# A hybrid encoder block on one core: the last product of the SwiGLU in parts of 3, 4, 4 pairs, x joined by accumulating DMA, and the final norm's two factors applied in one operation

## The chip, the cores and the metric

The kernel runs on one core of one Trainium2 chip. The metric is the device time of one execution, in microseconds (us), lower is better. Before the change the median of 3 executions is 1082.14 us (1081.68 to 1083.57).

The engines are named as in the profile: PE (TensorE, matmuls), PEld (its weight loads), DVE (VectorE), ACT (ScalarE), POOL (GpSimd) and SP (SyncE, which here only issues DMAs). Each engine works through its own queue in order. An instruction that waits holds up what stands behind it in that queue.

## The reference

One layer of a bidirectional encoder, 512 tokens of 1024 features in float32: a gated short convolution beside a retention mixer, merged and added to x, then the part that this change is about:

```
h2 = rmsnorm(x, g_ffn)
x  = x + (silu(h2 @ w_ff_gate) * (h2 @ w_ff_up)) @ w_ff_down     # 1024 -> 2816 -> 1024
return rmsnorm(x, g_final)      # x * rsqrt(mean(x*x) + 1e-6) * g_final
```

## The kernel before

**Products.** Every float32 operand is split into a high and a low part (`split`, L166 on ACT for the high, L167 on DVE for the low), and every product is three matmuls: high by high, high by low, low by high.

**The FFN.** x after the mixers lies in DRAM as `ydr` (512 x 1024), in four blocks of 128 rows (nb 0 to 3) and two halves of 512 columns. The 2816 inner features are 11 pairs of 2 x 128. For each pair, `pair` computes gate and up, and `gated` the SwiGLU. Both the products into and out of the inner features are done in a Strassen-like form, with seven block products instead of eight. For the last product these are a11, a12, s1, s2, s3, a22, s4 in this order (`FORMS` has the weight forms b11, b21, t1, t2, t3, t4, b22 that go with them). A form t is a sum of weight tiles, added on DVE (L239) and then split; b11, b21 and b22 are only split. A unit is the form of two pairs (1024 columns), or of one where the number is odd (512 columns); units are prefetched two ahead of the matmuls.

**Parts.** `FF_PARTS` cuts the last product into parts of 4, 4 and 3 pairs. After the first and the second part, `down(n)` runs the seven products of that part (`prod_tm`: for each unit, two blocks of 128 tokens, n pairs, 3 matmuls of 128x128 by 512 columns, L870), takes sums out of the PSUM banks with ACT copies (`snap`, L848) and DVE operations, and adds them to `ydr` in DRAM by accumulating DMAs from the POOL queue (`add_y`, L876).

**The last part** is written out after `down`. It loads `ydr` into SBUF as `y[0]` and `y[1]` (L914, two DMAs of 1 MB on SP's queue). The seven products follow. `to_y` (L946) adds a bank to y on DVE, L960 and L964 subtract a bank from y on DVE. The product s3 accumulates into the same two banks `a` as s2, and a22 into them after s3; so each waits for the read of `a` before it. When a block of rows has one half final, `early` squares and sums it on ACT (L923), multiplies it with g_final on DVE (L924) and prepares the mean (L930). The last two products take an `evict` function that runs after each of their two token blocks: `ev_a` for nb 2 and 3, `ev_d` for nb 0 and 1. It calls `to_y` and `store`: square and sum (L923), multiply with g_final (L924), mean plus EPS (L936, 128x1), power -0.5 on POOL (L938, 128x1), scale one half on ACT (L939) and the other on DVE (L940), and two DMAs to the output on SP's queue (L942).

**What sets the order.** The code gives the order of the work; the framework's scheduler puts the instructions into the engines' queues at build time and may move one ahead of others where it expects it to be ready. In the trace the load of g_final (L916) stands over 270 us before the code's place for it.

Of the kernel before, what the change touches and what calls it, by code (L numbers as in the profile page):

```python
# [12 lines left out]
F32 = mybir.dt.float32  # L13
F32R = mybir.dt.float32r
AF = mybir.ActivationFunctionType
ALU = mybir.AluOpType

P = 128
D = 1024
S = 512  # L20
KD = D // P
NB = S // P
# [5 lines left out]
EPS = 1e-6  # L28
# [8 lines left out]
QH = CH // 2  # L37
NQ = NFB // 2

FF_PARTS = ((0, 4), (4, 4), (8, 3))  # L40

WARM = 8

# [5 lines left out]
def plan():  # L49
# [45 lines left out]
    def f(q, *names):  # L95
        for n in names:
            out.append(("q", ("f", q), n, 0, 4))

    f(0, "b11", "b21", "b12", "b22")
    f(1, "b11", "b21")  # L100
    for q0, n in FF_PARTS:
        for q in range(max(q0, 1), q0 + n):
# [36 lines left out]
def block_kernel(ctx: ExitStack, tc: tile.TileContext, xT, xtok, wpack, wquad, cols, decs, rot, g_ffn, g_final, out):  # L139
    nc = tc.nc  # L140
# [5 lines left out]
    small = ctx.enter_context(tc.tile_pool(name="small", bufs=4))  # L146
# [7 lines left out]
    def bigtile(dt=F32, n=4):  # L154
        return big.tile([P, n, 512], dt, tag="big", name="big", padded_shape=[P, 4, 512])

    def t512(dt=F32):
        return tmp.tile([P, 512], dt, tag="t512", name="t512")

    def bank():  # L160
        return psum.tile([P, 512], F32, tag="bank", name="bank")
# [97 lines left out]
    def take():  # L259
        if not ready:  # L260
            prefetch()
        x, units = ready.pop(0)
        while sum(len(u) for _, u in ready) < AHEAD and prefetch():
            pass
        return x, units
# [83 lines left out]
    mhalf = const.tile([P, 8], F32, name="mhalf")  # L349
# [49 lines left out]
    for k in range(8):  # L399
# [16 lines left out]
                            op0=ALU.mult, op1=ALU.add)  # L416
    for j in range(15, 0, -2):
# [3 lines left out]
                                   op0=ALU.mult, op1=ALU.mult)  # L421
# [57 lines left out]
    def do_scores(h, qk):  # L479
        tab = decay(h)  # L480
        p = (bigtile(F32R), bigtile(F32R))
        for mb in range(NB):
            ps = bank()
            for d in range(2):
                sl = slice(mb * P, (mb + 1) * P)
                mm3(ps, (qk[0][:, 2 + d, sl], qk[1][:, 2 + d, sl]), (qk[0][:, d, :], qk[1][:, d, :]),
                    d == 0, d == 1)
            t = t512()
            o = (3 - mb) * P
            nc.vector.scalar_tensor_tensor(out=t, in0=ps, scalar=QK ** -0.5, in1=tab[:, o:o + 512],  # L490
                                           op0=ALU.mult, op1=ALU.mult)
            split(t, p[0][:, mb, :], p[1][:, mb, :])
        return p
# [101 lines left out]
    for h in range(HEADS):  # L595
        p = do_scores(h, qk)
# [47 lines left out]
    y = [bigtile(), bigtile()]  # L644
# [6 lines left out]
    ydr = dram.tile([S, D], F32, name="ydr")  # L651
# [48 lines left out]
    for half in range(2):  # L700
        c = Chunk()
# [15 lines left out]

    part_of = {q: (q0, n) for q0, n in FF_PARTS for q in range(q0, q0 + n)}
    act = {}
# [82 lines left out]
    def begin(q, step):  # L802

        st = heads_of.setdefault(q, {})
        _, (w,) = take()
        if step == 0:
            st["a"] = bank()
            prod(w, XF[0, 0], st["a"], True)
            st["p1"] = t512()
            nc.scalar.copy(st["p1"], st["a"])  # L810
        else:
            b = bank()
            prod(w, XF[1, 0], b, True)
            g = st["p1"]
            nc.vector.tensor_tensor(out=g, in0=b, in1=g, op=ALU.add)
# [32 lines left out]
        nc.scalar.copy(t, ps)  # L848
        return t

    def prod_tm(n, name, pss, start, stop=False, evict=None):

        w = []
        for u in range(0, n, 2):
            _, (x,) = take()
            if evict is None:
                units = ((u, x),)
            else:
                w.append((u, x))
                if u + 2 < n:  # L860
                    continue
                units = w
            xh, xl = act[name]
            for tt in range(2):
                for u0, (wh, wl) in units:
                    for k in range(u0, min(u0 + 2, n)):
                        c = slice((k - u0) * 512, (k - u0 + 1) * 512)
                        sl = slice(tt * P, (tt + 1) * P)
                        for i, (l, r) in enumerate(((xh, wh), (xh, wl), (xl, wh))):
                            nc.tensor.matmul(pss[tt], l[:, k, sl], r[:, c], start=start and k == 0 and i == 0,  # L870
                                             stop=stop and k == n - 1 and i == 2, skip_group_check=True)
                if evict:
                    evict(tt)

    def add_y(t, nb, half):
        nc.gpsimd.dma_start(out=ydr[nb * P:(nb + 1) * P, half * 512:(half + 1) * 512], in_=t, accum_op=ALU.add)  # L876
# [1 line left out]
    def down(n):  # L878
        a, b, d = ([bank(), bank()] for _ in range(3))
        prod_tm(n, "a11", a, True)  # L880
        p1 = [snap(x) for x in a]
        prod_tm(n, "a12", b, True, True)
        for tt in range(2):
            nc.vector.tensor_tensor(out=p1[tt], in0=b[tt], in1=p1[tt], op=ALU.add)
            add_y(p1[tt], tt, 0)
        prod_tm(n, "s1", d, True)
        prod_tm(n, "s2", a, False)
        u2 = [snap(x) for x in a]
        prod_tm(n, "s3", a, False)
        u3 = [snap(x) for x in a]  # L890
        for tt in range(2):
            nc.vector.tensor_tensor(out=u3[tt], in0=d[tt], in1=u3[tt], op=ALU.subtract)
            add_y(u3[tt], 2 + tt, 1)
        prod_tm(n, "a22", a, False, True)
        for tt in range(2):
            add_y(snap(a[tt]), 2 + tt, 0)
        prod_tm(n, "s4", d, False, True)
        for tt in range(2):
            nc.vector.tensor_tensor(out=u2[tt], in0=d[tt], in1=u2[tt], op=ALU.subtract)
            add_y(u2[tt], tt, 1)  # L900
# [3 lines left out]
    begin(1, 1)  # L904
    for q0, n in FF_PARTS:
        for q in range(max(q0, 1), q0 + n):
# [3 lines left out]


    y = [bigtile(), bigtile()]
    for half in range(2):
        nc.sync.dma_start(y[half], ydr[:, half * 512:(half + 1) * 512].rearrange("(n p) c -> p n c", p=P))  # L914
    gf = rawp.tile([P, D], F32, tag="gains", name="gf", bufs=1)
    nc.sync.dma_start(gf, g_final)  # L916
    acs = [small.tile([P, 6], F32, tag="fin", name="fin") for _ in range(NB)]

    def square(nb, half):

        yt, ac = y[half][:, nb, :], acs[nb]
        sq = t512()
        nc.scalar.activation(sq, yt, AF.Square, accum_out=ac[:, half:half + 1])  # L923
        nc.vector.tensor_tensor(out=yt, in0=yt, in1=gf[:, half * 512:(half + 1) * 512], op=ALU.mult)  # L924

    def early(nb, half):

        square(nb, half)
        ac = acs[nb]
        nc.vector.tensor_scalar(out=ac[:, 3:4], in0=ac[:, half:half + 1], scalar1=1.0 / D, scalar2=EPS,  # L930
                                op0=ALU.mult, op1=ALU.add)

    def store(nb, half):
        square(nb, half)
        ac = acs[nb]
        nc.vector.scalar_tensor_tensor(out=ac[:, 4:5], in0=ac[:, half:half + 1], scalar=1.0 / D,  # L936
                                       in1=ac[:, 3:4], op0=ALU.mult, op1=ALU.add)
        nc.gpsimd.tensor_tensor(out=ac[:, 5:6], in0=ac[:, 4:5], in1=mhalf[:, 0:1], op=ALU.pow)  # L938
        nc.scalar.activation(y[0][:, nb, :], y[0][:, nb, :], AF.Copy, scale=ac[:, 5:6])  # L939
        nc.vector.tensor_scalar_mul(y[1][:, nb, :], y[1][:, nb, :], ac[:, 5:6])  # L940
        for h in (1, 0):
            nc.sync.dma_start(out[nb * P:(nb + 1) * P, h * 512:(h + 1) * 512], y[h][:, nb, :])  # L942

    def to_y(ps, nb, half):
        yt = y[half][:, nb, :]
        nc.vector.tensor_tensor(out=yt, in0=ps, in1=yt, op=ALU.add)  # L946

    a, b, d = ([bank(), bank()] for _ in range(3))
    prod_tm(n, "a11", a, True)
    for tt in range(2):  # L950
        to_y(a[tt], tt, 0)
    prod_tm(n, "a12", b, True, True)
    for tt in range(2):
        to_y(b[tt], tt, 0)
        early(tt, 0)
    prod_tm(n, "s1", d, True)
    prod_tm(n, "s2", a, False)
    for tt in range(2):
        yt = y[1][:, tt, :]
        nc.vector.tensor_tensor(out=yt, in0=yt, in1=a[tt], op=ALU.subtract)  # L960
    prod_tm(n, "s3", a, False)
    for tt in range(2):
        yt = y[1][:, 2 + tt, :]
        nc.vector.tensor_tensor(out=yt, in0=yt, in1=a[tt], op=ALU.subtract)  # L964
        to_y(d[tt], 2 + tt, 1)
        early(2 + tt, 1)

    def ev_a(tt):
        to_y(a[tt], 2 + tt, 0)
        store(2 + tt, 0)  # L970

    def ev_d(tt):
        to_y(d[tt], tt, 1)
        store(tt, 1)
    prod_tm(n, "a22", a, False, True, ev_a)
    prod_tm(n, "s4", d, False, True, ev_d)


def pack_weights(arrays):
# [60 lines left out]
```

## Time and profile before

| | us |
|---|---|
| median of 3 executions | 1082.14 |
| the profiled execution's own time | 1081.23 |
| its span, first to last instruction | 1079.4 |
| PE busy in the span | 1062.5 (98%) |
| DVE busy | 743.5 (69%) |
| ACT busy | 429.8 (40%) |
| POOL busy | 34.1 (3%) |

The span is the time between the first and the last instruction that the profiler saw; the own time has 1.8 us more around it. The mean granted TensorE clock is 0.997. A busy share over the whole span says little of the last 40 us, where other engines than PE can set the pace; those are read by themselves.

### The profile page before, as it was taken

To read this page: it belongs to the slowest core of one execution; us is meant where nothing else is said; L and a number is where in the kernel's file an instruction comes from. 1 tells how busy PE (TensorE), PEld (TensorE's weight loads), DVE (VectorE), ACT (ScalarE), POOL (GpSimd) and SP (SyncE) were. 2 spreads that over 40 slices of the span, in tenths; PEclk is the share of its full clock that TensorE was granted. 3 is DMA by queue.
4 is the path that set the end of the run, shared out by engine and by line. 5 is a ranking of instruction groups with operands and counts; after the bars stand their busy time and mean duration, and the time that the engine had idled before them with its cause. 6 is when DMAs were issued, how large, how long until landed. Compare 5 with 4: busy or idle time off the path is not lost. (4 is left out here: it accounts for less than half of the span.)

```text
span 1079.4 us, 13769 instructions
## 1 busy us (share of the span) xinstructions
PE 1062.5 (98%) x5560; PEld 913.8 (85%) x5560; DVE 743.5 (69%) x1012; ACT 429.8 (40%) x569; POOL 34.1 (3%) x50
## 2 busy tenths in 40 slices
PE   8999999999999999999999999999999999999995
PEld 7888888888888888888888888889998899989974
DVE  7846574757575746955364444459898979897997
ACT  7352244225222522222132323345555545554544
POOL 0000000000000000000000000000000100011001
PEclk9999999999999999999999999999999999999998
DMA  7322222212221322042323232922331942256402
GB/s 264 130 95 88 68 94 83 78 59 98 79 78 59 118 82 94 22 135 89 106 97 99 95 101 93 355 98 60 100 115 33 243 118 97 79 158 145 166 1 78
DMA packets 35727, 114.69 MB, mean 106 GB/s; under 512 B 4048, under 2 KB 4048, under 8 KB 35664
## 3 DMA queue, kind: packets, MB, share of 16 engines
q1 hardware_dynamic: 33360, 109.62, 30.4%
q0 software_dynamic: 2304, 4.20, 2.7%
q8 instruction: 43, 0.70, 0.3%
q14 instruction: 20, 0.16, 0.0%
HBM read 105.41 MB, written 8.39 MB: 105 GB/s over the span
## 5 line engine op out<-in xcount | busy, mean ns | idle before, releaser
L166 ACT CAST whi<-raw 128x1024 fp32r<-128x1024 f32 (+1 forms) x236 | 241.1, 1029 | 405.6 <-PE bank L281 136.8
L167 DVE TENSOR_TENSOR wlo<-raw,whi 128x1024 fp32r<-128x1024 f32 (+1 forms) x236 | 280.6, 1196 | 171.4 <-ACT whi L166 170.4
L281 PE MATMUL bank<-big,whi 128*128 128x512 f32 x640 | 249.0, 389 | 0.0
L280 PE MATMUL bank<-big,whi 128*128 128x512 f32 x640 | 249.0, 389 | 0.0
L282 PE MATMUL bank<-big,wlo 128*128 128x512 f32 x640 | 249.0, 389 | 0.0
L730 PE MATMUL bank<-xform,whi 128*128 128x256 f32 x1248 | 227.9, 284 | 1.2 <-ACT t L826 1.2
L730 PEld LDWEIGHTS bank<-xform,whi 128*128 128x128 f32 x1248 | 194.8, 192 | 4.4 <-ACT t L826 2.4
L730 PE MATMUL bank<-xform,wlo 128*128 128x256 f32 x624 | 175.6, 283 | 0.0
L281 PEld LDWEIGHTS bank<-big,whi 128*128 128x128 f32 x640 | 120.1, 188 | 25.0
L280 PEld LDWEIGHTS bank<-big,whi 128*128 128x128 f32 x640 | 120.1, 188 | 25.0
L282 PEld LDWEIGHTS bank<-big,wlo 128*128 128x128 f32 x640 | 120.1, 188 | 24.9
L280 PE MATMUL bank<-whi,big 128*128 128x512 f32 x304 | 118.3, 391 | 1.9 <-ACT big L169 1.6
L730 PEld LDWEIGHTS bank<-xform,wlo 128*128 128x128 f32 x624 | 119.4, 192 | 0.0
L281 PE MATMUL bank<-wlo,big 128*128 128x512 f32 x304 | 118.4, 389 | 0.4 <-DVE wlo L167 0.4
L282 PE MATMUL bank<-whi,big 128*128 128x512 f32 x304 | 118.2, 389 | 0.0
L870 PE MATMUL bank<-whi,big 128*128 128x512 f32 x308 | 96.3, 392 | 1.5 <-DVE big L960 0.9
L166 ACT CAST big<-t 128x512 fp32r<-128x512 f32 (+1 forms) x92 | 53.7, 593 | 99.8 <-DVE t L475 28.6
L239 DVE TENSOR_TENSOR raw<-raw 128x1024 f32<-128x1024 f32 x64 | 75.0, 1184 | 0.4
L870 PEld LDWEIGHTS bank<-whi,big 128*128 128x128 f32 x308 | 57.7, 188 | 15.3 <-ACT whi L166 1.4
L280 PEld LDWEIGHTS bank<-whi,big 128*128 128x128 f32 x304 | 57.0, 188 | 14.3 <-ACT big L169 1.9
L281 PEld LDWEIGHTS bank<-wlo,big 128*128 128x128 f32 x304 | 57.1, 188 | 12.6 <-DVE wlo L167 0.9
L282 PEld LDWEIGHTS bank<-whi,big 128*128 128x128 f32 x304 | 57.1, 188 | 11.9
(145 smaller groups left out, 919.5 us busy)
## 6 DMA issues: line engine op xcount, KB each, us to landing
raw<-wpack SPq DMA_DIRECT2D x118, 512.0 KB, 3.7
raw<-wquad SPq DMA_DIRECT2D x64, 512.0 KB, 4.3
ydr<-t POOLq DMA_DIRECT2D x16, 256.0 KB, 5.7
big<-xtok SPq DMA_DIRECT2D x2, 1024.0 KB, 6.3
ydr<-big SPq DMA_DIRECT2D x8, 256.0 KB, 2.1
big<-ydr SPq DMA_DIRECT2D x2, 1024.0 KB, 4.9
y<-big SPq DMA_DIRECT2D x8, 256.0 KB, 2.3
raw<-wpack SPq DMA_DIRECT2D x4, 256.0 KB, 6.0
```

The lines of the kernel that those rows point to most:

```text
L166: nc.scalar.copy(hi, src)
L167: nc.vector.tensor_tensor(out=lo, in0=src, in1=hi.bitcast(F32), op=ALU.subtract)
L239: nc.vector.tensor_tensor(out=t, in0=t, in1=raws[quad, more, u][:, 0:n], op=ALU.add)
L280: nc.tensor.matmul(ps, lh, rh, start=first, stop=False)
L281: nc.tensor.matmul(ps, lh, rl, start=False, stop=False)
L282: nc.tensor.matmul(ps, ll, rh, start=False, stop=last)
L730: nc.tensor.matmul(o, l[:, c], r[:, k], start=start and s == 0 and k == 0 and i == 0, stop=stop and k == 3 and i == 2, skip_group_check=True)
L870: nc.tensor.matmul(pss[tt], l[:, k, sl], r[:, c], start=start and k == 0 and i == 0, stop=stop and k == n - 1 and i == 2, skip_group_check ...
```

## The change

`FF_PARTS` becomes 3, 4, 4 pairs. In the last part only rows nb 2 and 3 of the first half are loaded from `ydr`. For the six other sums that were added to y on DVE (a11 for nb 0 and 1, s2 for nb 0 and 1, s3 for nb 2 and 3), the new `snap_y` has ACT write the bank to the y tile (with its sign), and a DMA from the POOL queue adds the rows of `ydr` to it. `to_y` adds a bank to y, squares and sums on ACT, and prepares the mean on DVE. The multiplication with g_final (L924) is gone, but for one (`gain(1, 0)`): `store` multiplies with the norm's factor and with g_final in one DVE operation for each half, and for nb 1's first half, which has g_final already, ACT scales. The product s4 computes its second token block in two parts of 256 columns (`cuts`), each followed by its `to_y`.

```diff
-FF_PARTS = ((0, 4), (4, 4), (8, 3))
+FF_PARTS = ((0, 3), (3, 4), (7, 4))
...
+                for c0, c1 in zip(cuts[tt], cuts[tt][1:]):
+                    for u0, (wh, wl) in units:
...
+                                nc.tensor.matmul(pss[tt][:, c0:c1], l[:, k, sl], r[:, c],
...
+                    if evict:
+                        evict(tt, c0, c1)
...
-    for half in range(2):
-        nc.sync.dma_start(y[half], ydr[:, half * 512:(half + 1) * 512].rearrange("(n p) c -> p n c", p=P))
+    for nb in (2, 3):
+        nc.sync.dma_start(y[0][:, nb, :], rows(nb, 0))
...
+    def snap_y(ps, nb, half, sign):
+        yt = y[half][:, nb, :]
+        nc.scalar.activation(yt, ps, AF.Copy, scale=sign)
+        nc.gpsimd.dma_start(out=yt, in_=rows(nb, half), accum_op=ALU.add)
+
+    def to_y(ps, nb, half, c0=0, c1=512, last=False):
+        yt, ac, i = y[half][:, nb, c0:c1], acs[nb], sums[nb]
+        nc.vector.tensor_tensor(out=yt, in0=ps[:, c0:c1], in1=yt, op=ALU.add)
         sq = t512()
-        nc.scalar.activation(sq, yt, AF.Square, accum_out=ac[:, half:half + 1])
+        nc.scalar.activation(sq[:, 0:c1 - c0], yt, AF.Square, accum_out=ac[:, i:i + 1])
+        if i == 0:
+            nc.vector.tensor_scalar(out=ac[:, 4:5], in0=ac[:, 0:1], scalar1=1.0 / D, scalar2=EPS,
+                                    op0=ALU.mult, op1=ALU.add)
+        else:
+            nc.vector.scalar_tensor_tensor(out=ac[:, 4 + i:5 + i], in0=ac[:, i:i + 1], scalar=1.0 / D,
+                                           in1=ac[:, 3 + i:4 + i], op0=ALU.mult, op1=ALU.add)
+        sums[nb] += 1
+        if last:
+            nc.gpsimd.tensor_tensor(out=ac[:, 7:8], in0=ac[:, 4 + i:5 + i], in1=mhalf[:, 0:1], op=ALU.pow)
+
+    def gain(nb, half):
+        yt = y[half][:, nb, :]
         nc.vector.tensor_tensor(out=yt, in0=yt, in1=gf[:, half * 512:(half + 1) * 512], op=ALU.mult)
...
-        nc.scalar.activation(y[0][:, nb, :], y[0][:, nb, :], AF.Copy, scale=ac[:, 5:6])
-        nc.vector.tensor_scalar_mul(y[1][:, nb, :], y[1][:, nb, :], ac[:, 5:6])
-        for h in (1, 0):
-            nc.sync.dma_start(out[nb * P:(nb + 1) * P, h * 512:(h + 1) * 512], y[h][:, nb, :])
+    def store(nb, scaled=()):
+        for half in (1, 0):
+            yt = y[half][:, nb, :]
+            if half in scaled:
+                nc.scalar.activation(yt, yt, AF.Copy, scale=acs[nb][:, 7:8])
+            else:
+                nc.vector.scalar_tensor_tensor(out=yt, in0=yt, scalar=acs[nb][:, 7:8],
+                                               in1=gf[:, half * 512:(half + 1) * 512],
+                                               op0=ALU.mult, op1=ALU.mult)
+            nc.sync.dma_start(out[nb * P:(nb + 1) * P, half * 512:(half + 1) * 512], yt)
...
     prod_tm(n, "a11", a, True)
     for tt in range(2):
-        to_y(a[tt], tt, 0)
+        snap_y(a[tt], tt, 0, 1.0)
...
     prod_tm(n, "s2", a, False)
     for tt in range(2):
-        yt = y[1][:, tt, :]
-        nc.vector.tensor_tensor(out=yt, in0=yt, in1=a[tt], op=ALU.subtract)
+        snap_y(a[tt], tt, 1, -1.0)
     prod_tm(n, "s3", a, False)
     for tt in range(2):
-        yt = y[1][:, 2 + tt, :]
-        nc.vector.tensor_tensor(out=yt, in0=yt, in1=a[tt], op=ALU.subtract)
+        snap_y(a[tt], 2 + tt, 1, -1.0)
         to_y(d[tt], 2 + tt, 1)
-        early(2 + tt, 1)
+    gain(1, 0)
...
-    prod_tm(n, "s4", d, False, True, ev_d)
+    prod_tm(n, "s4", d, False, True, ev_d, cuts=((0, 512), (0, 256, 512)))
```

## Rows read from the trace of the kernel before

**Rows 1.** The page: span, then busy time and share of each engine.
```profile
span 1079.4 us, 13769 instructions
...
PE 1062.5 (98%) x5560; PEld 913.8 (85%) x5560; DVE 743.5 (69%) x1012; ACT 429.8 (40%) x569; POOL 34.1 (3%) x50
```

**Rows 2.** Two stretches, L870's matmuls alone; columns in the first line.
```profile
core 0: us, PE busy (x) PEld busy (x), PEclk, DMA share, GB/s
946.40:979.90 33.50, 33.50 (x149) 27.58 (x147) 1.00 0.72 170
1049.15:1068.80 19.65, 17.55 (x74) 13.21 (x73) 1.00 0.00 0
```

**Rows 3.** PE's timeline: start, length; in brackets idle time before, and releaser.
```profile
1049.98 0.73 PE L870 MATMUL bank<-whi,big 128*128 128x512 f32 x2 [0.40 <-ACT whi L166]
1051.31 0.50 PE L870 MATMUL bank<-wlo,big 128*128 128x512 f32 x1 [0.59 <-DVE wlo L167]
...
1056.14 0.47 PE L870 MATMUL bank<-whi,big 128*128 128x512 f32 x1 [0.91 <-DVE big L960]
...
1060.70 0.47 PE L870 MATMUL bank<-whi,big 128*128 128x512 f32 x1 [0.19 <-DVE big L964]
...
1068.75 0.39 PE L870 MATMUL bank<-whi,big 128*128 128x512 f32 x1
```

**Rows 4.** One stretch: busy us (count) of PE, PEld, DVE, ACT, POOL.
```profile
1039.00:1069.20 30.20, 28.04 (x119) 21.41 (x117) 28.67 (x47) 14.30 (x27) 0.56 (x1) 1.00 0.00 1
```

**Rows 5.** DVE's timeline in the last part's products.
```profile
1046.38 1.28 DVE L946 TENSOR_TENSOR big<-bank,big 128x512 f32<-128x512 f32 x2
...
1048.71 0.68 DVE L924 TENSOR_TENSOR big<-big,gf 128x512 f32<-128x512 f32 x1
...
1055.32 1.28 DVE L960 TENSOR_TENSOR big<-big,bank 128x512 f32<-128x512 f32 x2
```

**Rows 6.** Groups by line and shape, 700 to 1080 us: count, busy us, mean ns.
```profile
L769 DVE TENSOR_TENSOR t<-t,t 128x256 f32<-128x256 f32 x33 | 13.0, 417 | 0.0
...
L848 ACT COPY t<-bank 128x512 f32<-128x512 f32 x16 | 9.0, 585 | 8.0 <-PE bank L870 8.0
...
L677 DVE SCALAR_TENSOR_TENSOR t<-big,ac,gb 128x512 f32<-128x512 f32 x8 | 5.7, 748 | 2.4 <-POOL ac L673 2.4
...
L166 ACT CAST big<-t 128x256 fp32r<-128x256 f32 x11 | 4.4, 404 | 0.3 <-DVE t L753 0.3
...
L940 DVE TENSOR_SCALAR big<-big,fin 128x512 f32<-128x512 f32 x4 | 1.9, 486 | 1.6 <-POOL fin L938 1.6
```

**Rows 7.** Chain of waits, matmuls of 256 columns: start, length, count.
```profile
1033.24 5.96 PE bank L730 x48
```

**Rows 8.** DVE's timeline after the last matmul.
```profile
1071.15 0.49 DVE L940 TENSOR_SCALAR big<-big,fin 128x512 f32<-128x512 f32 x1 [0.44 <-POOL fin L938]
...
1071.62 0.68 DVE L946 TENSOR_TENSOR big<-bank,big 128x512 f32<-128x512 f32 x1
...
1073.72 0.69 DVE L924 TENSOR_TENSOR big<-big,gf 128x512 f32<-128x512 f32 x1 [0.88 <-ACT t L923]
...
1075.14 0.48 DVE L940 TENSOR_SCALAR big<-big,fin 128x512 f32<-128x512 f32 x1 [0.66 <-POOL fin L938]
```

**Rows 9.** ACT's timeline at the last square.
```profile
1072.99 0.61 ACT L923 ACTIVATE t<-big 128x512 f32<-128x512 f32 x1
```

**Rows 10.** POOL's timeline: the powers of the first and the last row block.
```profile
1068.64 0.88 POOL L938 TENSOR_TENSOR fin<-fin,mhalf 128x1 f32<-128x1 f32 x1 [86.10 <-DVE fin L936]
...
1074.56 0.54 POOL L938 TENSOR_TENSOR fin<-fin,mhalf 128x1 f32<-128x1 f32 x1 [2.24 <-DVE fin L936]
```

**Rows 11.** Tile `ydr`, 832 to 834 us: two accumulating DMAs, issue to landing.
```profile
DMA to landing us min/median/max: 3.9/4.5/5.0
```

**Rows 12.** The same, six issued 969 to 982 us beside weight loads.
```profile
DMA to landing us min/median/max: 4.6/6.9/7.6
```

**Rows 13.** PE's timeline at pair 10, columns as in rows 3.
```profile
1028.49 0.50 PE L730 MATMUL bank<-xform,whi 128*128 128x256 f32 x2 [1.17 <-ACT t L826]
```

More of the change, by code (lines that the diff above doesn't have):

```diff
@@ L849, in snap, with prod_tm @@
         return t
-    def prod_tm(n, name, pss, start, stop=False, evict=None):
+    def prod_tm(n, name, pss, start, stop=False, evict=None, cuts=((0, 512), (0, 512))):
         w = []
@@ L864, in prod_tm @@
             for tt in range(2):
[L865 to L873, printed above, removed]
+                sl = slice(tt * P, (tt + 1) * P)
+                for c0, c1 in zip(cuts[tt], cuts[tt][1:]):
+                    for u0, (wh, wl) in units:
+                        for k in range(u0, min(u0 + 2, n)):
+                            c = slice((k - u0) * 512 + c0, (k - u0) * 512 + c1)
+                            for i, (l, r) in enumerate(((xh, wh), (xh, wl), (xl, wh))):
+                                nc.tensor.matmul(pss[tt][:, c0:c1], l[:, k, sl], r[:, c],
+                                                 start=start and k == 0 and i == 0,
+                                                 stop=stop and k == n - 1 and i == 2, skip_group_check=True)
+                    if evict:
+                        evict(tt, c0, c1)
     def add_y(t, nb, half):
@@ L912, in block_kernel, with rows @@
     y = [bigtile(), bigtile()]
-    for half in range(2):
-        nc.sync.dma_start(y[half], ydr[:, half * 512:(half + 1) * 512].rearrange("(n p) c -> p n c", p=P))
+    def rows(nb, half):
+        return ydr[nb * P:(nb + 1) * P, half * 512:(half + 1) * 512]
+    for nb in (2, 3):
+        nc.sync.dma_start(y[0][:, nb, :], rows(nb, 0))
     gf = rawp.tile([P, D], F32, tag="gains", name="gf", bufs=1)
     nc.sync.dma_start(gf, g_final)
-    acs = [small.tile([P, 6], F32, tag="fin", name="fin") for _ in range(NB)]
@@ L919, in square @@
-    def square(nb, half):
-        yt, ac = y[half][:, nb, :], acs[nb]
-        sq = t512()
-        nc.scalar.activation(sq, yt, AF.Square, accum_out=ac[:, half:half + 1])
-        nc.vector.tensor_tensor(out=yt, in0=yt, in1=gf[:, half * 512:(half + 1) * 512], op=ALU.mult)
[L926 to L938, printed above, removed]
-        nc.scalar.activation(y[0][:, nb, :], y[0][:, nb, :], AF.Copy, scale=ac[:, 5:6])
-        nc.vector.tensor_scalar_mul(y[1][:, nb, :], y[1][:, nb, :], ac[:, 5:6])
-        for h in (1, 0):
-            nc.sync.dma_start(out[nb * P:(nb + 1) * P, h * 512:(h + 1) * 512], y[h][:, nb, :])
@@ L944, in to_y @@
-    def to_y(ps, nb, half):
-        yt = y[half][:, nb, :]
-        nc.vector.tensor_tensor(out=yt, in0=ps, in1=yt, op=ALU.add)
+    acs = [small.tile([P, 8], F32, tag="fin", name="fin") for _ in range(NB)]
+    sums = [0] * NB
+    def snap_y(ps, nb, half, sign):
[5 more added lines that the diff above has]
+        nc.vector.tensor_tensor(out=yt, in0=ps[:, c0:c1], in1=yt, op=ALU.add)
+        sq = t512()
+        nc.scalar.activation(sq[:, 0:c1 - c0], yt, AF.Square, accum_out=ac[:, i:i + 1])
[8 more added lines that the diff above has]
+            nc.gpsimd.tensor_tensor(out=ac[:, 7:8], in0=ac[:, 4 + i:5 + i], in1=mhalf[:, 0:1], op=ALU.pow)
@@ L954, in block_kernel @@
         to_y(b[tt], tt, 0)
-        early(tt, 0)
     prod_tm(n, "s1", d, True)
@@ L958, in block_kernel, with ev_a, ev_d @@
     for tt in range(2):
-        yt = y[1][:, tt, :]
-        nc.vector.tensor_tensor(out=yt, in0=yt, in1=a[tt], op=ALU.subtract)
+        snap_y(a[tt], tt, 1, -1.0)
     prod_tm(n, "s3", a, False)
     for tt in range(2):
-        yt = y[1][:, 2 + tt, :]
-        nc.vector.tensor_tensor(out=yt, in0=yt, in1=a[tt], op=ALU.subtract)
+        snap_y(a[tt], 2 + tt, 1, -1.0)
         to_y(d[tt], 2 + tt, 1)
-        early(2 + tt, 1)
[L968 to L974, printed above, removed]
+    gain(1, 0)
+    def ev_a(tt, c0, c1):
+        to_y(a[tt], 2 + tt, 0, last=True)
+        store(2 + tt)
+    def ev_d(tt, c0, c1):
+        to_y(d[tt], tt, 1, c0, c1, last=c1 == 512)
+        if c1 == 512:
+            store(tt, (0,) if tt else ())
     prod_tm(n, "a22", a, False, True, ev_a)
-    prod_tm(n, "s4", d, False, True, ev_d)
+    prod_tm(n, "s4", d, False, True, ev_d, cuts=((0, 512), (0, 256, 512)))
 def pack_weights(arrays):
```

## The prediction, made before the change was run

> **What bounds the kernel now.** I read the page first. PE is busy 1062.5 of 1079.4 us [rows 1], so a change outside PE pays only where PE has gaps or is done. So I looked for those places, first by stretches, then in PE's timeline. In the last product of the middle part, 148 matmuls begin in 33.50 us (the row's 149 less the one begun before its edge), 0.226 us each, without a gap [rows 2]. In the last part only 73 begin in 19.65 us, up to the last at 1068.75 [rows 2, 3]. At the same pace they need 16.5 us: 3.1 us are lost, in four gaps that the timeline marks, idle 0.40, 0.59, 0.91 and 0.19 us plus the refilling of the pipeline [rows 3]. Their releasers are a high half of ACT, a low half of DVE, and the subtractions L960 and L964. What they share is DVE: it is busy 28.67 of the 30.20 us there, ACT 14.30 [rows 4]. The third place is the end. PE's last matmul starts at 1068.75 and ends 0.39 us later, at 1069.14 [rows 3]; the span ends at 1079.4. Of these 10.3 us, 2.48 pass until DVE starts the last add, L946 at 1071.62 [rows 8], because a scaling L940 of an earlier row stood before it in DVE's queue, waiting for POOL. Another 3.52 us pass until the last power is there and the last L940 starts at 1075.14 [rows 8], and 4.26 us are scaling, DMA and closing.
>
> **PE's gaps in the last part.** Up to the last two products, DVE loses ten operations of 128x512: two adds of a11, two L960, two L964, four L924. Each starts 0.64 us after the one before it (two in 1.28 us [rows 5]), 6.4 us in all; one `gain` of 0.68 us is added. So 5.7 of 28.67 us of DVE work go. In their place ACT gets six copies of 0.585 us [rows 6], 3.5 us; ACT was busy less than half of the time [rows 4]. The last part then has the form of `down(4)`: ACT frees the banks `a` after s2 and s3, and units are 1024 columns, so that two units ahead cover 24 x 0.226 = 5.4 us of PE. That is the stretch with no gap [rows 2], where DVE even had two adds more. I take all 3.1 us as gained; the bounds are 0 (new waits keep DVE late) and 3.1, since no more is lost there. The part of 3 pairs moves to the front; it takes along the short cover but not L924 or L946's y adds. I take 0 there; at worst it inherits the first two gaps, 1.0 us idle [rows 3]. A fourth gap, 1.17 us at pair 10, waits for ACT's copy L826 [rows 13]; the work there is the same, so I leave it, with 0 to -1.2 us for another queue order.
>
> **s4 cut in two.** Twelve matmuls of 512 columns become 24 of 256. The matmuls of 256 in `prod` go at 5.96/48 = 0.124 us [rows 7]; 24 x 0.124 = 2.98 against 12 x 0.226 = 2.71: **+0.25 us** on PE, nothing beside it.
>
> **From PE's end to the last add.** It was 2.48 us. Now a row of 512 needs, from bank to both scalings done: add 0.68 [rows 8]; square with its sum 0.73 (1072.99 to L924's start at 1073.72 [rows 8, 9]); the small operation and handoff to POOL 0.23 (1074.33 to 1074.56, the same as L924's end to POOL's start [rows 8, 10]); power 0.88, as in the row with DVE busy [rows 10]; two scalar_tensor_tensor, mean 0.748 with some overlap [rows 6], together 1.4. That is 3.9 us. Banks become ready 2.7 us apart, so rows pile up if DVE goes strictly in the order of the code. With PE's end as 0, nb 0's bank is ready at -2.98. If its add runs at once, its scalings end at +0.95. If nb 3's scalings run first (bank at -5.7, done -1.8), it is +2.1; if nb 2's too, +3.4. If the last add is placed before nb 0's scalings it runs at once. So 0.1 to 3.4 us; I take 1.2, near the case where each add runs when ready, because before, too, adds were moved ahead of scalings and only the last came behind some. **-1.3 us**.
>
> **From the last add to the power.** It was 3.52 us, with ACT and DVE also held by nb 0's scaling (L939, then the square at 1072.99 [rows 9]) and L924 0.6 us ahead of L936. Now: add of 256 columns 0.417, the nearest row of that width [rows 6]; the square 0.73 less the difference between 512 and 256 columns on ACT, 0.61 against 0.404 [rows 6, 9], 0.52; 0.23; power 0.54, as with DVE idle [rows 10]; handoffs 0.05: 1.76 us. By the rows at 512 throughout it would be 2.2; that is the upper bound, 1.6 the lower. **-1.75 us**.
>
> **After the power.** L940 of 0.486 becomes a scalar_tensor_tensor of 0.748 [rows 6]; the first store leaves 0.25 us later, and the second follows it: **+0.25 us** (0 to 0.3). The factor's second multiplication costs nothing else: L924 was its own operation before.
>
> **The moved DMAs.** SP issues two loads of 256 KB in place of two of 1 MB, at the same place and long before their use. POOL issues six accumulating DMAs; POOL had been idle for 86 us before its first power [rows 10], so only their landing counts. In the trace such DMAs land 3.9 to 5.0 us after issue when nothing else runs [rows 11], and 4.6 to 7.6 us beside weight loads [rows 12]; both write DRAM, none writes SBUF, so 3.9 to 7.6 is the bound and 4.5 the value I take, since the weight loads are done by then. For a11 the sum is used after a12: the second bank is copied 0.7 us after a11, issued and landed by 5.3, and a12 takes 5.4 us. No wait. For s2 the use is two products later. For s3 see the second rival.
>
> **Sum**: -3.1 + 0.25 - 1.3 - 1.75 + 0.25 = -5.65 us. The profiled execution took 1081.23 us, 1079.4 of it span: 1075.6. The median is 0.9 us above that execution, so on the median's scale 1082.14 - 5.65 = **1076.5 us**. Its own range, by the bounds of the small terms (-1.2 for pair 10, 1.0 for the first part, 0.1 to 1.7 for the last add), is 1074 to 1078.5.
>
> **Rivals.**
>
> *DVE takes the last rows in the order of the code.* For it: in the trace L940 waits for POOL in front of the last add. Against it: it takes both nb 2's and nb 3's scalings before nb 0's add. The last add then comes at +3.4: -5.65 + 2.2 = -3.45, 1078.7 us.
>
> *DVE waits for the DMA after s3.* `to_y` for nb 2 and 3 of the second half follows s3 at once, and the low halves of b22, which s4 needs, stand behind it in the code. With a landing of 4.5 us nb 3's rows are complete 0.7 + 0.1 + 4.5 = 5.3 us after s3; then add 0.64, gain 0.64, two low halves of about 1.15 (twice the 0.6 us spacing of 512 columns): 8.9 us, while a22 covers 5.4. PE stalls 3.5 us before s4: -2.15, 1080.0 us. Against it: b22's halves depend on neither and can be queued ahead. The Trainium skill, page "DMA: Bandwidth & Descriptors", section "Anatomy of one DMA — SWDGE (gpsimd) path", gives about 2.0 us plus bytes over 436 GB/s, an estimate of 2.6 us for 256 KB, and a stall of about 1.6; rows 11 measure 3.9 to 5.0 into DRAM, which differs, and no row shows SBUF as the target.
>
> *Slower: the accumulating DMAs into SBUF land late.* The same wait, but at both places where DVE stands before a DMA. With landing L the stall before s4 is L - 1.0. After a12 DVE waits to 0.8 + L, then two adds and the two halves of t2's first unit, 3.6 us, against s1's end at 10.8: a stall of L - 6.4. Against -5.65 both together decide from L = 6.6 us on. That is inside the 7.6 us of rows 12, and a DMA that reads DRAM and SBUF and writes SBUF was never timed here. At 9 us it is 8.0 + 2.6 = 10.6 us: 1087 us. Against it: no weight loads run then.
>
> *The change does not do what it says for PE.* The gaps come from the order of the queues, not from DVE's load, and stay: -2.55, 1079.6 us; the same if the first part takes as much as the last gives.
>
> **Chances.** Forecast 0.50; order of the code 0.15; wait after s3 0.16; late landing 0.10; gaps stay 0.09. A difference of 0.2% (2.2 us) is about what measurement can tell from none: faster below 1080.0, slower above 1084.3. Faster: 0.48 + 0.13 + 0.08 + 0 + 0.05 = 0.74. Same: 0.02 + 0.02 + 0.07 + 0.03 + 0.04 = 0.18. Slower: 0.01 + 0.07 = 0.08. The range leaves out the late landing and the bottom: 1073.8 to 1081.
>
> **What would show it.** Right: from the start of the last part's last six products no gap of PE over 0.2 us; no L960, L964; DVE's adds after a12 and s3 not idle for a DMA; from PE's end to the last add under 1.7 us, from there to the last power under 2 us. Wrong: idle time of DVE released by a DMA of y, with PE waiting for a low half of b22 or t2 behind it; the scalings of nb 2 standing before the add of nb 0; landing times of y's accumulating DMAs over 6.6 us; new gaps in the part of 3 pairs.

## The result, and the profile after

The change made the kernel slower, by 0.3%: 1084.94 us, median of 15 runs (1083.29 to 1086.02), against 1081.75 us (15 runs, 1080.64 to 1083.57) before. The ratio is 1.0028, 95% interval 1.0020 to 1.0036. The forecast was 1076.5 us, with a range of 1073.8 to 1081: the sign was wrong.

The profiled execution took 1085.06 us, 1083.3 of it span. The page of the kernel after, its span, its busy times and its group of the last products' matmuls (line, engine, operation, tiles, count, then busy time, mean ns, idle time before and its releaser):

```profile
span 1083.3 us, 13802 instructions
...
PE 1066.4 (98%) x5572; PEld 917.8 (85%) x5572; DVE 738.8 (68%) x1004; ACT 431.6 (40%) x574; POOL 38.8 (4%) x56
...
L872 PE MATMUL bank<-whi,big 128*128 128x512 f32 (+1 forms) x316 | 99.2, 393 | 5.8 <-DVE big L936 3.8
```

Against [rows 1] PE is busy 3.9 us longer with only 12 more matmuls, and has new idle time. The matmul's line was L870 and is now L872; the add of a bank to y was L946 and is now L936. Where the time goes shows in PE's timeline of the kernel after (start, length, and in brackets the idle time before and its releaser):

```profile
1051.23 0.39 PE L872 MATMUL bank<-whi,big 128*128 128x512 f32 x1
1053.57 0.50 PE L872 MATMUL bank<-whi,big 128*128 128x512 f32 x1 [1.95 <-ACT big L930]
...
1054.78 0.63 PE L872 MATMUL bank<-wlo,big 128*128 128x512 f32 x1
1055.21 1.05 PE L872 MATMUL bank<-whi,big 128*128 128x512 f32 x2
...
1070.24 0.28 PE L872 MATMUL bank<-whi,big 128*128 128x256 f32 x1
1074.34 0.39 PE L872 MATMUL bank<-whi,big 128*128 128x256 f32 x1 [3.82 <-DVE big L936]
...
1076.45 0.41 PE L872 MATMUL bank<-whi,big 128*128 128x256 f32 x1
```

The four short gaps of [rows 3] are gone, and two long ones are marked in the last part: one of 1.95 us before s3 (between s2 and s3, whose banks ACT's copy L930 has to free), and one of 3.82 us in the cut half of s4, between its two parts. DVE's timeline, same columns, shows what stands behind both:

```profile
1041.86 0.69 DVE L936 TENSOR_TENSOR big<-bank,big 128x512 f32<-128x512 f32 x1 [1.12 <-DMA big<-ydr]
1044.24 0.69 DVE L936 TENSOR_TENSOR big<-bank,big 128x512 f32<-128x512 f32 x1 [1.69 <-DMA big<-ydr]
...
1049.51 2.36 DVE L239 TENSOR_TENSOR raw<-raw 128x1024 f32<-128x1024 f32 x2
...
1064.28 1.29 DVE L936 TENSOR_TENSOR big<-bank,big 128x512 f32<-128x512 f32 x2 [3.72 <-DMA big<-ydr]
1066.60 0.69 DVE L936 TENSOR_TENSOR big<-bank,big 128x512 f32<-128x512 f32 x1 [1.03 <-DMA big<-ydr]
...
1069.73 1.41 DVE L959 SCALAR_TENSOR_TENSOR big<-big,fin,gf 128x512 f32<-128x512 f32 x2 [0.75 <-POOL fin L947]
...
1071.94 1.41 DVE L959 SCALAR_TENSOR_TENSOR big<-big,fin,gf 128x512 f32<-128x512 f32 x2 [0.72 <-POOL fin L947]
1073.27 1.02 DVE L936 TENSOR_TENSOR big<-bank,big 128x512 f32<-128x512 f32 x2
...
1076.95 0.42 DVE L936 TENSOR_TENSOR big<-bank,big 128x256 f32<-128x256 f32 x1
...
1078.77 0.75 DVE L959 SCALAR_TENSOR_TENSOR big<-big,fin,gf 128x512 f32<-128x512 f32 x1 [0.66 <-POOL fin L947]
```

Four adds wait for an accumulating DMA into y (`big<-ydr`), 7.6 us together, at exactly two places: after a12 (1.12 and 1.69) and after s3 (3.72 and 1.03). The adds of [rows 5] wait for nothing. The tile's view of `ydr` in the kernel after has the time from issue to landing for the two pairs of DMAs that these adds need (issued 1037 to 1039.5 us, then 1060 to 1062.5):

```profile
DMA to landing us min/median/max: 3.7/4.6/5.6
...
DMA to landing us min/median/max: 3.8/4.2/4.7
```

How much of PE's work lies between a11 and a12's use shows in three stretches of the kernel after, L872's matmuls alone (columns as in [rows 2]; the last row's 13 include one begun before its edge):

```profile
1018.00:1025.30 7.30, 2.85 (x10) 1.75 (x10) 1.00 0.01 2
1031.00:1037.40 6.40, 6.22 (x26) 4.92 (x27) 1.00 0.01 1
1037.40:1040.10 2.70, 2.70 (x13) 2.24 (x12) 1.00 0.13 20
```

ACT's timeline carries the first wait over to PE:

```profile
1037.15 1.08 ACT L930 ACTIVATE big<-bank 128x512 f32<-128x512 f32 x2
...
1050.84 2.18 ACT L166 CAST whi<-raw 128x1024 fp32r<-128x1024 f32 x2 [4.15 <-DVE raw L239]
1052.92 1.08 ACT L930 ACTIVATE big<-bank 128x512 f32<-128x512 f32 x2
```

Stretches of the kernel after (length, then busy us and count of PE, PEld, DVE, ACT, POOL, the granted clock, DMA share, GB/s):

```profile
1037.00:1070.00 33.00, 30.91 (x132) 24.92 (x131) 20.52 (x28) 16.16 (x28) 5.84 (x7) 0.95 0.31 48
1045.00:1051.00 6.00, 5.86 (x26) 4.53 (x25) 6.00 (x8) 1.82 (x4) 0.00 (x0) 1.00 0.00 0
1054.40:1057.70 3.30, 3.30 (x9) 2.61 (x8) 1.56 (x2) 0.54 (x1) 1.17 (x2) 0.50 0.73 104
```

Read together: DVE's load fell, from 28.67 of 30.2 us [rows 4] to 20.52 of 33. (The second stretch belongs to a part of 4 pairs and leaves out the adds behind 1070, so the two do not measure the 5.7 us of the forecast.) But DVE loses its free time at the wrong place. It stands idle for 2.8 us before the DMAs of a11, and is then late: from 1045 to 1051 it is busy without a break. Among what is late are the sums of raw weights L239 at 1049.51. ACT's high halves wait 4.15 us for them, and behind these in ACT's queue stands the copy L930 that frees s2's bank. So PE stops before s3, and then runs for 3.4 us at the lower granted clock (0.50, the 1.2 GHz level), where matmuls begin 0.43 us apart (1054.78 and 1055.21). In the chain of waits of the kernel after (start, length, what), the two longest pieces from 1053 us on are this stretch and the second wait:

```profile
1053.57 7.38 PE bank L872 x24
...
1061.86 4.72 DMA big<-ydr
```

The 24 matmuls of s3 take 7.38 us; at the pace of [rows 2], 0.226 us each, they take 5.4.

### The profile page after: what moved, and what is told of

It is laid out like the page before. It is cut to its first block, busy times and chain, and to the rows that moved or that the text cites. A ratio compares the mean times of both kernels' runs of the same rounds, so it can differ in the third digit from the quotient of the medians.

```text
span 1083.3 us, 13802 instructions
## 1 busy us (share of the span) xinstructions
PE 1066.4 (98%) x5572; PEld 917.8 (85%) x5572; DVE 738.8 (68%) x1004; ACT 431.6 (40%) x574; POOL 38.8 (4%) x56
## 5 line engine op out<-in xcount | busy, mean ns | idle before, releaser
L280 PE MATMUL bank<-whi,big 128*128 128x512 f32 x304 | 118.8, 392 | 2.1 <-ACT big L169 2.1
L282 PE MATMUL bank<-whi,big 128*128 128x512 f32 x304 | 118.6, 391 | 0.0
L872 PE MATMUL bank<-whi,big 128*128 128x512 f32 (+1 forms) x316 | 99.2, 393 | 5.8 <-DVE big L936 3.8
L872 PEld LDWEIGHTS bank<-whi,big 128*128 128x128 f32 x316 | 60.1, 192 | 20.1 <-DVE big L936 4.0
L239 DVE TENSOR_TENSOR raw<-raw 128x1024 f32<-128x1024 f32 x64 | 75.1, 1186 | 0.9 <-DMA raw<-wquad 0.4
L280 PEld LDWEIGHTS bank<-whi,big 128*128 128x128 f32 x304 | 57.5, 189 | 14.2 <-ACT big L169 2.4
L282 PEld LDWEIGHTS bank<-whi,big 128*128 128x128 f32 x304 | 57.3, 189 | 12.1
```

Of the source, the lines that this page charges most:

```text
L239: nc.vector.tensor_tensor(out=t, in0=t, in1=raws[quad, more, u][:, 0:n], op=ALU.add)
L280: nc.tensor.matmul(ps, lh, rh, start=first, stop=False)
L282: nc.tensor.matmul(ps, ll, rh, start=False, stop=last)
L872: nc.tensor.matmul(pss[tt][:, c0:c1], l[:, k, sl], r[:, c], start=start and k == 0 and i == 0, stop=stop and k == n - 1 and i == 2, skip_g ...
```

## The experiments

The runs came in three groups (e1 to e4, e5 to e8, e9 and e10), each beside runs of the kernel before on the same chip; these had medians of 1081.75, 1081.64 and 1081.76 us, so medians of different groups are compared directly below. My theory after the result was that the two places where DVE stands before a DMA cost the time, and that the cut of s4 adds its same-bank wait. The rival was that the end is set by DVE's queue of row blocks, whatever PE does before.

**e1_parts_alone.** The kernel before, with the parts alone.

```diff
-FF_PARTS = ((0, 4), (4, 4), (8, 3))
+FF_PARTS = ((0, 3), (3, 4), (7, 4))
```

> The kernel before with parts of 3, 4, 4 pairs and nothing else. Theory W (waits): the loss comes from two new waits, the DMA that DVE waits for and the second half of s4 that waits for the first half's add; then the parts alone cost about nothing: 1081 to 1083 us, PE's gaps in the last part smaller than the 3.1 us of before, about 1 us of new gaps in the first part of 3 pairs. Theory P (parts): the longer last part and the short first part lose the time themselves: 1084 to 1085 us.

Measured: 1079.07 us, ratio 0.9973 [0.9963, 0.9983]. Faster by 2.7 us, so both expectations missed. From 1039 us on PE's timeline of e1 has one marked gap in place of the four of [rows 3]; the second line is its last matmul:

```profile
1059.06 0.47 PE L870 MATMUL bank<-whi,big 128*128 128x512 f32 x1 [0.43 <-ACT whi L166]
...
1069.84 0.39 PE L870 MATMUL bank<-whi,big 128*128 128x512 f32 x1
```

The longer last part (4 pairs) closes three of the four gaps by itself. But most of the 2.7 us is not PE's. The FFN's first matmul in PE's timeline of the kernel before, of e1 and of e2, and then e1's last add in DVE's timeline:

```profile
730.05 0.48 PE L730 MATMUL bank<-xform,whi 128*128 128x256 f32 x2
...
732.24 0.48 PE L730 MATMUL bank<-xform,whi 128*128 128x256 f32 x2
...
729.88 0.48 PE L730 MATMUL bank<-xform,whi 128*128 128x256 f32 x2
...
1070.84 0.68 DVE L946 TENSOR_TENSOR big<-bank,big 128x512 f32<-128x512 f32 x1
```

From the FFN's first matmul to the end of the last, PE takes 339.1 us in the kernel before and 338.0 in e1, so 1.1 us are gained there. The rest lies behind PE: e1's last add starts 0.6 us after PE's end, where it was 2.48.

**e2_two_factors.** The kernel after without the accumulating DMAs (y is loaded whole, DVE adds and subtracts as before) and without the cut. What remains over e1 is the norm's two factors in one operation, and the order of operations that goes with it.

```diff
-    for nb in (2, 3):
-        nc.sync.dma_start(y[0][:, nb, :], rows(nb, 0))
+    for half in range(2):
+        nc.sync.dma_start(y[half], ydr[:, half * 512:(half + 1) * 512].rearrange("(n p) c -> p n c", p=P))
...
-        nc.scalar.activation(yt, ps, AF.Copy, scale=sign)
-        nc.gpsimd.dma_start(out=yt, in_=rows(nb, half), accum_op=ALU.add)
+        if sign > 0:
+            nc.vector.tensor_tensor(out=yt, in0=ps, in1=yt, op=ALU.add)
+        else:
+            nc.vector.tensor_tensor(out=yt, in0=yt, in1=ps, op=ALU.subtract)
...
-    prod_tm(n, "s4", d, False, True, ev_d, cuts=((0, 512), (0, 256, 512)))
+    prod_tm(n, "s4", d, False, True, ev_d)
```

> The changed kernel without the accumulating DMAs (x is loaded by SP and joined by DVE adds as before) and without the cut of s4: parts and the two factors in one operation remain. Theory W: no DVE wait for a DMA, no bank wait: 1078 to 1080.5 us, faster than before by the L924 work taken off DVE. Theory T (two factors): two scalar_tensor_tensor of 0.75 us for each row block fill DVE at the end and delay the last add; then 1082 or more.

Measured: 1077.85 us, 0.9962 [0.9948, 0.9976]; 1.2 us below e1, though the two intervals overlap. The profiles agree: from the FFN's first matmul to the end of the last PE takes 337.1 us, 0.9 less than in e1. DVE's timeline of e2 (L931 adds a11, L938 the later banks) has no wait for a DMA:

```profile
1037.82 0.69 DVE L931 TENSOR_TENSOR big<-bank,big 128x512 f32<-128x512 f32 x1
1039.02 1.37 DVE L938 TENSOR_TENSOR big<-bank,big 128x512 f32<-128x512 f32 x2
...
1066.24 0.68 DVE L938 TENSOR_TENSOR big<-bank,big 128x512 f32<-128x512 f32 x1
1067.79 0.68 DVE L938 TENSOR_TENSOR big<-bank,big 128x512 f32<-128x512 f32 x1
```

The first two lines also show how soon a12's banks are ready: both adds have started within 1.9 us of the start of a11's second add, without waiting.

**e3_no_cut.** The kernel after without the cut; so e2 and e3 differ only in how the six sums join y: added by DVE, or copied by ACT and added by the accumulating DMAs.

```diff
-    prod_tm(n, "s4", d, False, True, ev_d, cuts=((0, 512), (0, 256, 512)))
+    prod_tm(n, "s4", d, False, True, ev_d)
```

> The changed kernel with s4 in one part of 512 columns again, accumulating DMAs kept. Theory W: the 4.0 us gap of PE before the last half goes; the last add still stands late in DVE's queue, so 2 to 3 us of it come back: 1081.5 to 1083 us; the gap of 2.2 us before s3 and the low clock after it stay. Rival Q (DVE's queue alone sets the end, the cut costs nothing): 1084.5 us or more.

Measured: 1084.45 us, 1.0023 [1.0015, 1.0032]. The DMAs cost 6.6 us against e2, with intervals far apart; the cut costs 0.5 here, which the intervals do not tell from nothing. The 2 to 3 us expected back did not come, and the rival held: PE ends 4.7 us earlier than in the kernel after (1072.20 against 1076.86), and the time hardly moves. PE's timeline of e3, from pair 10's gap to the last matmul:

```profile
1020.39 0.50 PE L872 MATMUL bank<-wlo,big 128*128 128x512 f32 x1 [1.37 <-DVE wlo L167]
...
1046.52 0.50 PE L872 MATMUL bank<-wlo,big 128*128 128x512 f32 x1 [0.52 <-DVE fin L940]
...
1053.97 0.50 PE L872 MATMUL bank<-whi,big 128*128 128x512 f32 x1 [1.93 <-ACT big L930]
...
1071.81 0.39 PE L872 MATMUL bank<-whi,big 128*128 128x512 f32 x1
```

The last add L936 of e3 starts at 1075.21, 3.0 us after PE's end.

**e4_cut_two_banks.** The kernel after, with the two column halves of a cut product in a PSUM bank each (for s1 and s4).

```diff
+                                ps = pss[tt][c0 // 256] if isinstance(pss[tt], tuple) else pss[tt]
...
-    a, b, d = ([bank(), bank()] for _ in range(3))
+    a, b = ([bank(), bank()] for _ in range(2))
+    d = [bank(), (bank(), bank())]
...
-    prod_tm(n, "s1", d, True)
+    prod_tm(n, "s1", d, True, cuts=halves)
```

> The changed kernel with the two column halves of s1 and s4 (second token block) in two PSUM banks of their own. Theory W, that the second half waits because DVE still has to read the first half out of the same bank: the 4.0 us gap goes although the cut stays, 1081.5 to 1083 us. Rival: the halves wait for something else (the weights, the order of PE's queue): the gap stays, 1085 us.

Measured: 1084.35 us, 1.0024 [1.0016, 1.0033]. In PE's timeline the 3.82 us gap is gone, as expected; the last matmul comes 6 us earlier than in the kernel after, and the gap before s3 stays:

```profile
1054.01 0.50 PE L873 MATMUL bank<-whi,big 128*128 128x512 f32 x1 [1.93 <-ACT big L931]
...
1070.49 0.28 PE L873 MATMUL bank<-whi,big 128*128 128x256 f32 x1
```

So the wait came from the shared bank: the second half's matmuls wait until DVE has read the first half. The Trainium skill, page "PSUM — Partial Sum Buffer", section "PSUM bank collisions raise a hardware error", says that accesses of different engines have to be kept apart by bank and quadrant, not by address; the traces agree in that the kernel waits 3.82 us with one bank and not with two. What would happen without the wait no run shows. The time, expected at 1081.5 to 1083, is that of e3, as the last add still comes at 1075.38, held by DVE's queue.

**e5_adds_later.** e3, with a12's adds placed behind s2's copies in the code.

```diff
     prod_tm(n, "a12", b, True, True)
-    for tt in range(2):
-        to_y(b[tt], tt, 0)
     prod_tm(n, "s1", d, True)
     prod_tm(n, "s2", a, False)
     for tt in range(2):
         snap_y(a[tt], tt, 1, -1.0)
+    for tt in range(2):
+        to_y(b[tt], tt, 0)
```

> The changed kernel without the cut, and with the two adds of a12 (nb 0 and 1) queued after s2 instead of right after a12, so that DVE does not stand before the DMA of a11's sums. Theory D (DVE's queue stands before the accumulating DMA): DVE's two idle times there (1.7 and 1.5 us) go, and with them PE's gap of 2.4 us before s3, the gap of 1 us before it and the low clock behind it: 1080 to 1081.5 us against 1084.45 without the cut. Rival A (the ACT copies and POOL's DMA issues are what costs, wherever DVE's adds stand): 1083.5 us or more.

Measured: 1080.02 us, 0.9984 [0.9975, 0.9993]: 4.4 us faster than e3, as expected. In DVE's timeline of e5 the wait after a12 is gone, and the one after s3 is the same:

```profile
1045.81 1.28 DVE L936 TENSOR_TENSOR big<-bank,big 128x512 f32<-128x512 f32 x2
...
1060.34 1.29 DVE L936 TENSOR_TENSOR big<-bank,big 128x512 f32<-128x512 f32 x2 [3.58 <-DMA big<-ydr]
```

PE's timeline of e5 has no marked gap after that at pair 10, and the granted clock is 1.00 from 1046 to 1068 us:

```profile
1020.83 0.50 PE L872 MATMUL bank<-wlo,big 128*128 128x512 f32 x1 [1.37 <-DVE wlo L167]
...
1067.58 0.39 PE L872 MATMUL bank<-whi,big 128*128 128x512 f32 x1
```

From pair 10's gap to the last matmul e5 needs 46.75 us, e3 51.42: PE ends 4.67 us sooner. Two gaps make 2.45 of them and eight matmuls at 0.43 in place of 0.226 us 1.6; the rest, 0.6, I put down to refilling the pipeline after the gaps. The DMA after s3 is issued that much sooner too, and with it the row blocks at the end.

**e6_s3_by_dve.** e3, with s3's two sums loaded by SP and subtracted on DVE, so that the wait after s3 goes.

```diff
+    for nb in (2, 3):
+        nc.sync.dma_start(y[1][:, nb, :], rows(nb, 1))
...
-        snap_y(a[tt], 2 + tt, 1, -1.0)
+        yt = y[1][:, 2 + tt, :]
+        nc.vector.tensor_tensor(out=yt, in0=yt, in1=a[tt], op=ALU.subtract)
```

> The changed kernel without the cut, and with s3's sums for nb 2 and 3 joined as before (rows of x loaded by SP, two DVE subtractions), so that only the DMA wait after s3 is taken away. Theory D: DVE's idle 3.7 and 1.1 us after s3 go, the adds of the last rows run when their banks are ready, the early gap before s3 stays: 1081.5 to 1083 us. Rival A: 1084 us or more.

Measured: 1083.75 us, 1.0014 [1.0005, 1.0023]: 0.7 below e3, within the intervals, and less than expected (1081.5 to 1083). So taking this wait of 3.7 and 1.1 us off DVE brings at most a small part of the loss. In e6, as in e7 below, the four row blocks then follow each other at 3.7 us on DVE; what the wait costs with another order at the end this run does not show.

**e7_no_dma_wait.** e5 and e6 together: no add of DVE waits for a DMA; the DMAs for a11 and s2 remain.

```diff
-    for tt in range(2):
-        to_y(b[tt], tt, 0)
     prod_tm(n, "s1", d, True)
...
+    for tt in range(2):
+        to_y(b[tt], tt, 0)
...
-        snap_y(a[tt], 2 + tt, 1, -1.0)
+        nc.vector.tensor_tensor(out=yt, in0=yt, in1=a[tt], op=ALU.subtract)
```

> Both of these together: four of the six accumulating DMAs stay, but DVE never stands before one. Theory D: as fast as with no accumulating DMA at all (1077.85) or a little faster, since four DVE operations are on ACT: 1077 to 1078.5 us. Rival A: 1081 us or more.

Measured: 1079.82 us, 0.9983 [0.9974, 0.9992]. 1.3 us above the upper end that I expected, and 2.0 above e2. DVE's timeline of e7 shows the rest; these are the adds that finish the first, third and fourth row block:

```profile
1061.54 0.69 DVE L938 TENSOR_TENSOR big<-bank,big 128x512 f32<-128x512 f32 x1 [0.31 <-PE bank L872]
...
1068.94 0.68 DVE L938 TENSOR_TENSOR big<-bank,big 128x512 f32<-128x512 f32 x1
...
1072.56 0.68 DVE L938 TENSOR_TENSOR big<-bank,big 128x512 f32<-128x512 f32 x1
```

They come 3.7 us apart, strictly one row block after the other, where PE delivers a bank every 2.7 us. The last comes 2.9 us after PE's end (1069.27 + 0.39), in e2 0.8 after it (1066.57 + 0.39), because there the last two adds, 1.55 us apart, stand ahead of nb 0's scalings.

**e8_two_factors_cut.** e2 with the cut of s4 put back.

```diff
-    prod_tm(n, "s4", d, False, True, ev_d)
+    prod_tm(n, "s4", d, False, True, ev_d, cuts=((0, 512), (0, 256, 512)))
```

> The changed kernel without accumulating DMAs but with the cut of s4 (one bank, as changed). Where DVE is not late, the second half waits only for the first half's add and its handoff, 0.6 to 0.9 us of PE, and the last chain is 0.4 us shorter: 1077.5 to 1078.7 us against 1077.85 without the cut. Rival C (the cut costs its 4 us gap wherever it stands): 1081 us or more.

Measured: 1078.84 us, 0.9975 [0.9964, 0.9986]: 1.0 above e2, as medians; the intervals overlap. The gap in s4 is there without any accumulating DMA, longer than the 0.6 to 0.9 us expected and shorter than in the kernel after, where DVE's add of the first half stands later in its queue. PE's timeline of e8:

```profile
1069.14 0.39 PE L872 MATMUL bank<-whi,big 128*128 128x256 f32 x1 [1.65 <-DVE big L938]
```

**e9_early_gains** and **e10_early_gains_act.** e2 and e7, each with the halves that are ready early multiplied by g_final when DVE has time, and scaled on ACT at the end, so that a row block needs one scaling on DVE in place of two.

```diff
-    gain(1, 0)
+    for nb, half in ((0, 0), (1, 0), (2, 1), (3, 1)):
+        gain(nb, half)
...
-        store(2 + tt)
+        store(2 + tt, (1,))
...
-            store(tt, (0,) if tt else ())
+            store(tt, (0,))
```

> Parts and two factors without accumulating DMAs and without the cut, but only the late half of each row block is scaled by the two-factor operation on DVE; the early halves are multiplied with g_final before the last two products and scaled on ACT. Theory R (at the end one row block after the other goes through add, square, mean, power and two scalings, 3.7 us of DVE's queue each, against 2.7 us of PE): 0.7 us less for each row block, so the last add no longer waits for DVE's queue: 1075.5 to 1077.5 us against 1077.85. Rival (PE's end and the last chain set the time, not DVE's queue): 1077.5 to 1078.5, as without it, or more by the three added gains.

> The same scaling on the version with four accumulating DMAs that DVE never stands before (1079.82 us). There the last add came 2.9 us after PE's end, with the four row blocks strictly one after the other. Theory R: 2 to 3 us come back: 1076.8 to 1078 us. Rival (the rest is lost by ACT's copies and POOL's DMA issues): 1079.3 us or more.

Measured: e9 1077.94 us, 0.9968 [0.9956, 0.9981], no better than e2, so its rival held: there the last add was only 0.8 us behind PE. e10 1077.89 us, 0.9967 [0.9955, 0.9979]: 1.9 below e7, as expected. In DVE's timeline of e10 the row blocks follow each other at 3.0 us, near PE's 2.7 (again the first, third and fourth):

```profile
1061.64 0.68 DVE L938 TENSOR_TENSOR big<-bank,big 128x512 f32<-128x512 f32 x1
...
1067.71 0.68 DVE L938 TENSOR_TENSOR big<-bank,big 128x512 f32<-128x512 f32 x1
...
1070.67 0.68 DVE L938 TENSOR_TENSOR big<-bank,big 128x512 f32<-128x512 f32 x1
```

So nearly all of what e7 lost against e2 was DVE's queue at the end. e2, e9 and e10, all near 1077.9 us, are faster than both kernels.

## Why the prediction was wrong

As medians the change comes apart as follows: parts -2.7, two factors -1.2, accumulating DMAs +6.6, cut +0.5. The steps of the parts and of the DMAs stand outside the intervals, the other two do not. One profile of each, from the FFN's first matmul to the end of the span, gives nearly the same (349.4 us before, then 346.4, 345.4, 352.1 and 352.7): -3.0, -1.1, +6.7, +0.6. Of the 6.6 us the wait after a12 is 4.4 (e3 to e5), the wait after s3 0.2 (e5 to e7) and the rest, 2.0 (e7 to e2), nearly all DVE's queue at the end (e10).

**The step that failed** is the one on the moved DMAs: "For a11 the sum is used after a12: the second bank is copied 0.7 us after a11, issued and landed by 5.3, and a12 takes 5.4 us. No wait." Both halves of this were off. The landing was later: the two DMAs took 3.7 and 5.6 us against 4.5 taken, and the add that needs the second starts at 1044.24, 6.7 us after the end of a11's last matmul (about 1037.6) in place of 5.3. And the cover was not 5.4 us: PE's queue does not take a11 and a12 one after the other. Of their 48 matmuls 36 have begun by 1037.4 (10 among pair 10's, then 26), and ACT copies a11's banks from 1037.15 on. The trace does not label the products, so I infer it from that copy: a11's 24 end there, 12 of a12's 24 stand ahead of that end, and only the other 12 x 0.226 = 2.7 us lie behind it. e2's first two lines of DVE show a12's banks ready that early. So the sum came 4.0 us after the bank in place of 0.1 before it: 2.7 by the cover, 1.4 by the landing, and either alone would have made a wait. DVE, which had other work for a part of that time, stood idle for 2.8 us, and e5, which removes that wait alone, gives back 4.4 us. I had read the order of the products from the code and their durations from the trace, and not where the queue had mixed them.

**The second error** is how a wait on DVE is passed on. My third rival asked only when the low halves of t2 would be late for PE, and came to a stall of L - 6.4, nothing below a landing of 6.4 us. That sum has the same cover in it: with 2.7 us in place of 5.4 it gives L - 3.7, a stall already at the 4.5 us taken, and e3's line at 1046.52 has one of 0.52 us there. The longer stop, 1.95 us, came by a path through ACT that no rival had: DVE's sums of raw weights late, ACT's high halves behind them, and behind these the copy that frees s2's bank. "ACT frees the banks `a` after s2 and s3" was counted as help for PE; it also put ACT's queue, and through it DVE's, between s2 and s3. So the kernel was slower with landings of 5.6 us at most, under the 6.6 us that I gave as the threshold.

**The wait after s3** was seen (rival 2), with its size: 3.72 and 1.03 us on DVE. Its price was not the 3.5 us named: PE did not stop before s4 for the low halves in e5, and e6 gives 0.7 us against e3, e7 0.2 against e5, both with DVE's row blocks in the slow order at the end. That the halves of b22 can be queued ahead, the argument against it, was right.

**PE's gaps in the last part, -3.1.** Two thirds of the size are borne out, and the reason only in part. From the FFN's first matmul to the end of the last, PE gains 1.1 us by the parts alone (e1), with all of DVE's old adds, and 2.0 with the two factors as well (e2), which take most of the multiplications L924 off DVE. Moving DVE's sums to DMAs as well adds little: 2.2 us in e5 and 1.5 in e7. The other 1.9 us of e1 belong to the term "From PE's end to the last add", whose -1.3 the parts alone had already; why that add came sooner no run shows.

**s4 cut, +0.25, "nothing beside it".** It measured +0.5 and +1.0, which the intervals tell neither from 0.25 nor from nothing; but the wait of the second half for DVE's read of the same bank was missed, 3.82 us here and 1.65 in e8. It cost little in the kernel after because DVE's queue, not PE, held the end (e3).

**The end.** From the last add to the last scaling it took 1.82 us (1076.95 to 1078.77), against 1.76 forecast up to the power. From PE's end to the last add it took 0.1 us against 1.2 taken, but that is luck: PE ended 7.7 us later than in [rows 3], because the second part of s4 waited for the same DVE queue. Without the cut it is 3.0 us in e3, near the upper bound of 3.4, and 0.8 in e2. Rival 1, rows in the order of the code, is what the kernel after did: the scalings of nb 2 (1069.73) and of nb 3 (1071.94) stand before the add of nb 0 (1073.27), which the prediction names as a sign of being wrong. In e7, where nb 0's scalings stand before nb 1's add as well, this queue costs 2.0 us against e2, of which e10 gives back 1.9; the forecast for this rival was 2.2.

**What stays open** is the share of the lower clock within the 4.4 us. The eight slow matmuls cost PE 1.6 us; how much of that reaches the time is not shown. The lower clock is in the profiles of the kernel after and e3, and not in those of e4 and e6, which have the same gap. e3 and e4 have the same time, but e4's cuts add operations to DVE's queue that may have used up the gain.

## What to carry to other kernels

An accumulating DMA that spares an engine an add turns into a wait on that same engine if the sum is next used there: count the cover between issue and use in the order of the engine's queue, not of the code. When an in-order engine stands before a DMA, price everything queued behind it and follow each item into the other engines' queues, down to what frees PE's banks. And before giving a gain to the largest part of a change, ask whether its smallest (here three numbers in a tuple) has it already, and in the trace of that one, where the time came out: here more of it behind PE than on PE.

## What the runs showed of the hardware

Two accumulating DMAs of 256 KB into SBUF, issued 0.6 us apart on POOL's queue (a11's), landed 3.7 to 4.6 and 5.5 to 6.3 us after issue in the seven kernels that have them, with no weight loads beside them. Pairs issued 1.1 to 1.4 us apart took 3.6 to 3.8 and 4.5 to 5.0. The pair into DRAM, issued 1.7 us apart, took 3.9 and 5.0 [rows 11]. So SBUF as the target is neither clearly faster nor slower, and of two close behind each other the second lands later.

PE's granted clock went to 0.50 for 3.4 us shortly after a gap of 1.95 us in the kernel after and after one of 1.93 in e3, while it stayed at 1.00 after gaps of 1.93 in e4 and 1.94 in e6, whose stretches before were the same products. A gap of that length alone thus does not say whether the clock falls.
